# Mean square by a constant weight matrix and row-wide Newton steps in the norms, one batch of indexer scores per query block

## Chip, cores, metric

The kernel runs on one core of one Trainium2 chip. The metric is the device time of a launch in microseconds, as the median over several runs.

## Reference, cut to what matters

Two layers (`DEPTH = 2`) of a hybrid decoder trunk on 256 positions of width 1024, all in float32. Each layer takes a root-mean-square norm, projects, mixes in three branches, adds, takes a second norm and runs a gated feed-forward net:

```python
def rms_norm(x, g):
    r = lax.rsqrt(jnp.mean(xf * xf, axis=-1, keepdims=True) + NORM_EPS)
    return xf * r * g
...
h = rms_norm(x, norm1_g)
proj = h @ w_in                        # q, k, v, iq, ik, iw, a, c, g
y_attn = dsa_attention(q, k, v, iq, ik, iw) @ w_attn_out
y_conf = silu(layer_norm(conv31(a_val * sigmoid(a_gate)), ...)) @ w_conf_out
y_sc = (c_b * conv3(c_c * c_x)) @ w_sc_out
x = x + (sig(g0)*y_conf + sig(g1)*y_attn + sig(g2)*y_sc) @ w_o
u = causal_dwconv(rms_norm(x, norm2_g) @ w_up, ffn_conv_w) + ffn_conv_b
x = x + (silu(u_gate) * u_val) @ w_down
```

The attention picks 64 keys per query by the scores of a small indexer, in query blocks of 128:

```python
rel = relu(einsum('bthd,bsd->bths', iqb, ik))     # 8 indexer heads of width 64
score = einsum('bths,bth->bts', rel, iwb)         # then causal mask and top-k
```

So there are three norms over the 1024 features in a layer: here called a (ahead of `w_in`), c (the LayerNorm of the convolution branch) and b (ahead of `w_up`); the layers are 0 and 1.

## The kernel before, in words

Activations lie feature-major: eight tiles of 128 features by 256 positions (`xres` is the residual). The weights come from memory once, as a stream of 128x2048 chunks (`raw`, 3 buffers), each cut in two halves of 128x1024. Every product is float32 in two parts: ScalarE casts a half to its high part (`wh`, L426), VectorE subtracts that from the whole for the low part (`wl`, L383, both with 6 buffers), and TensorE makes three passes for each 128x128 tile: high times high, low times high, high times the low part of the activations. A matmul is 128x128 weights against 128x256 activations, and 24 of them consume one half. The stages of a layer follow the stream: A (convolution branch, eight pairs of column blocks), IQ, KX, V, Q (indexer and attention projections), C and CB (short convolution), S, then G (gates), T, F (branch outputs), O (`w_o`), U (`w_up`, 22 pairs) and N (`w_down`). The other TensorE work (transposes, indexer scores, attention, norms) is full-precision float32 and is slipped in between these.

The first pairs behind a norm don't wait for it. A pair of stage A or U is multiplied with the un-normalised `xgh`, `xgl` (gain times `xres`) and scaled afterwards (`deferred`, tiles `dA`, `dU`), for the number of pairs that `NDEF` gives: A0 5, A1 3, U0 5, U1 3. From then on the normalised tiles `hh` (high, ScalarE) and `hl` (low, VectorE) are read, which `finish` makes one feature tile at a time from `h = xres * gain * r` on VectorE. At the very start the first two pairs of A are done feature tile by feature tile while the input arrives, and the weights of the first two chunks are split in pieces of 128x512.

`r`, the inverse square root of the mean square plus epsilon, is made by `rsqrt_rows` (L565): TensorE takes the squares `sq` as weights against one column of `avg` (a constant 128x128 matrix of 1/1024), which gives the mean square `ms` with positions on partitions, 128x2. VectorE adds epsilon and takes three Newton steps on 128x2 (`newton_ops`, twelve operations with the shift and the start value, tiles `tv`, `ty`, `tt`, `r2`). TensorE then spreads the result over all partitions, with `r2` broadcast as weights against the identity (`pr`, L572), and ScalarE copies that to `r`. The profile gives a product of 128x128 weights in full precision as four records for two matmuls.

The indexer (loop from L882): for each query block `b` and each half `hq` of the eight heads, four score matmuls go into two banks `is` of two heads each, ScalarE takes the ReLU, and VectorE adds the weighted heads to `sc`. Two such batches per block, four per layer.

What sets the order: nothing is issued in program order. A planner (`Plan`) holds all operations with a cost in ns, the engine and a due time (`G.due`, in most places the running time `clk` of TensorE's stream, shifted by constants), and a list scheduler takes on each engine, when it comes free by these costs, the ready operation with the earliest due time. Operations marked hot (names that begin with a letter of `HOT = "abcqk"`, so all norms) go ahead of others that are ready up to 200 ns sooner. The casts and lows of a weight half are due 9000 ns ahead of their matmuls. Each engine then executes its list in that order; a buffer is handed on when its last reader is planned to be done. So a changed cost moves the order of operations far from the place that was edited.

The lines that matter: L366 issues every matmul, L383 a two-tensor operation of VectorE (`vtt`), L390 one with a scalar and a tensor (`vstt`), L398 and L400 one with a tensor and immediate scalars (`vts`), L421 an activation, L426 a cast.

Of the kernel before, what the change touches and what calls it, by code (L numbers as in the profile page):

```python
# [11 lines left out]
I32 = mybir.dt.int32  # L12
AF = mybir.ActivationFunctionType
ALU = mybir.AluOpType
PSUM = bass.MemoryType.PSUM

P = 128
D = 1024
S = 256
# [6 lines left out]
EPS = 1e-6  # L26
# [110 lines left out]
def ap_of(x):  # L137
    return x.ap() if isinstance(x, View) else x
# [198 lines left out]
def trunk(ctx: ExitStack, tc: tile.TileContext, xt: bass.AP, wst: bass.AP, prm: bass.AP,  # L337
# [7 lines left out]
    G = Plan()  # L345
    clk = {"t": 0.0}

    def width(v):
        if isinstance(v, View) and not v.whole:
            return v.n  # L350
        raise ValueError

    def pe(mms, due=None):
        outs, ins, cost = {}, {}, 0.0
        for o, l, r, st, sp, n, full, kw in mms:
            outs[id(o)] = o
            ins[id(l)] = l
            ins[id(r)] = r
            cost += max(4 * (n / 2.4 + 1.2), 218) if full else max(n, 256) / 2.4 + 2.4

        def fn():
            for o, l, r, st, sp, n, full, kw in mms:
                if kw == "t":
                    nc.tensor.transpose(ap_of(o), ap_of(l), ap_of(r))
                else:
                    nc.tensor.matmul(ap_of(o), ap_of(l), ap_of(r), start=st, stop=sp, skip_group_check=bool(kw))  # L366

        G.add("pe", fn, list(outs.values()), list(ins.values()), cost, due=due)
        return cost

    def mm(o, l, r, st, sp, n, full=False, kw=None):
        return (o, l, r, st, sp, n, full, kw)
# [4 lines left out]
    def psum(v):  # L377
        return isinstance(v, View) and v.buf.tag in BANKS

    def vtt(o, a, b, op, n=None):  # L380
        n = n or width(o)
        c = 62 if psum(a) or psum(b) or psum(o) else 66
        G.add("dve", lambda: nc.vector.tensor_tensor(ap_of(o), ap_of(a), ap_of(b), op=op), [o], [a, b], (c + n) / 0.96)  # L383

    def vstt(o, a, s, b, op0, op1, n=None):
        n = n or width(o)
        c = 62 if psum(a) or psum(b) or psum(o) else 66
        if not isinstance(s, float):
            c += 58
        G.add("dve", lambda: nc.vector.scalar_tensor_tensor(ap_of(o), ap_of(a), ap_of(s), ap_of(b), op0=op0, op1=op1),  # L390
              [o], [a, s, b], (c + n) / 0.96)

    def vts(o, a, s1, s2, op0, op1=None, n=None):
        n = n or width(o)

        def fn():
            if op1 is None:
                nc.vector.tensor_scalar(ap_of(o), ap_of(a), s1, None, op0=op0)  # L398
            else:
                nc.vector.tensor_scalar(ap_of(o), ap_of(a), s1, s2, op0=op0, op1=op1)  # L400

        G.add("dve", fn, [o], [a], (62 + n) / 0.96 if psum(a) else (66 + n / 2) / 0.96)

    def act(o, i, f, scale=None, bias=None, accum=None, n=None):
        n = n or width(o)
        cost = n / 1.2 + (51 if psum(i) else 94)
        kw = {}
        ins = [i]
        outs = [o]
        for k, v in (("scale", scale), ("bias", bias)):  # L410
            if v is not None:
                kw[k] = v
                ins.append(v)
                cost += 93
        if accum is not None:
            kw["accum_out"] = accum
            outs.append(accum)
            cost += 93

        def fn():  # L420
            nc.scalar.activation(ap_of(o), ap_of(i), f, **{k: ap_of(v) for k, v in kw.items()})  # L421

        G.add("act", fn, outs, ins, cost, func=f)
# [16 lines left out]
    def t2(name, dt=F32):  # L440
        return G.buf([P, 2, S], "m2", name, dt)

    def u1(name, dt=F32):
        return G.buf([P, S], "b1", name, dt)

    def t1r(name):
        return G.buf([P, S], "rr", name)
# [68 lines left out]
    avg = G.buf([P, P], "avg", "avg")  # L516

    def const(n):
        o, w = CCOL[n]
        return csb[:, o:o + w]  # L520

    ident = const("ident")
# [15 lines left out]
    for k in range(KD):  # L538
        r, src = (r0, src0) if k < 4 else (r1, src1)
# [8 lines left out]
    def newton_ops(v, y, yi, t, n):  # L548
        vts(yi, v.bitcast(I32), 1, None, ALU.logical_shift_right, n=n)
        vts(yi, yi, -1.0, float(0x5F3759DF), ALU.mult, ALU.add, n=n)  # L550
        cur = yi.bitcast(F32)
        for _ in range(3):
            vtt(t, cur, cur, ALU.mult, n=n)
            vstt(t, t, -0.5, v, ALU.mult, ALU.mult, n=n)
            vstt(y, t, 1.5, cur, ALU.add, ALU.mult, n=n)
            cur = y

    def rsqrt(ss, n, scale, name, keep):
        v = G.buf([P, n], "tv", f"tv{name}")
        yi = G.buf([P, n], "ty", f"ty{name}", I32)  # L560
        t = G.buf([P, n], "tt", f"tt{name}")
        vts(v, ss, scale, EPS, ALU.mult, ALU.add, n=n)
        newton_ops(v, keep, yi, t, n)

    def rsqrt_rows(sq, name):  # L565
        G.hot = name[0] in HOT
        ms = G.buf([P, 2], "pa", f"ms{name}")
        pe([mm(ms[:, b:b + 1], sq[:, b * P:(b + 1) * P], avg[:, 0:1], True, True, 1, True) for b in range(2)])
        r2 = G.buf([P, 2], "r2", f"r2{name}")
        rsqrt(ms, 2, 1.0, name, r2)  # L570
        pr = G.buf([P, S], "pa", f"pr{name}")
        pe([mm(pr[:, b * P:(b + 1) * P], r2[:, b:b + 1].to_broadcast([P, P]), ident, True, True, P, True)  # L572
            for b in range(2)])
        r = t1r(f"r{name}")
        act(r, pr, AF.Copy)
        G.hot = False
        return r

# [176 lines left out]
    for l in range(DEPTH):  # L755
# [38 lines left out]
        ikT = G.buf([P, S], "ikT", f"ikT{l}")  # L794
# [7 lines left out]
        pss = tok(f"IQ{l}", xh, xl, 512, 2)  # L802
        iq = iqb[:, 0:4, :].rearrange("p (b u) d -> p b (u d)", b=2)
        iqT = iqb[:, 4:8, :]
        for b in range(2):
            act(iqb[:, 2 * b:2 * b + 2, :], pss[b].rearrange("p (u d) -> p u d", u=2), AF.Copy)
        pss = tok(f"KX{l}", xh, xl, KX, 2)
# [44 lines left out]
        for g in range(4):  # L852
# [9 lines left out]
            n = g - 1  # L862
# [14 lines left out]
        def spend(ns):  # L877
            paced["t"] += ns * PACE
            G.due = paced["t"]

        for b in range(2):
            nk = (b + 1) * P  # L882
            one = (66 + nk) / 0.96
            sc = G.buf([P, nk], f"sc{b}", f"sc{l}_{b}")
            cur = caus[b]
            for hq in range(2):
                pss = [G.buf([P, 2, nk], "pq", f"is{l}_{b}_{hq}_{i}") for i in range(2)]
                g = []
                for u in range(2):
                    for i in range(2):  # L890
                        q = slice(i * 64, (i + 1) * 64)
                        g.append(mm(pss[i][:, u, :], iqT[q, 2 * hq + u, b * P:(b + 1) * P], ikT[q, :nk],
                                    True, True, nk, True))
                pe(g)
                for i in range(2):
                    rl = G.buf([P, 2, nk], "rel", f"rel{l}_{b}_{hq}_{i}")
                    act(rl, pss[i], AF.Relu)
                    for u in range(2):
                        h = 4 * hq + 2 * u + i
                        vstt(sc, rl[:, u, :], iws[:, b, h:h + 1], cur, ALU.mult, ALU.add)  # L900
                        cur = sc
                        spend(one)
            for r in range(TOPK // 8):
                m8 = G.buf([P, 8], "m8", f"m8{l}_{b}_{r}")
                G.add("dve", lambda m8=m8, sc=sc: nc.vector.max(ap_of(m8), ap_of(sc)), [m8], [sc], one)
                G.add("dve", lambda m8=m8, sc=sc: nc.vector.match_replace(ap_of(sc), ap_of(m8), ap_of(sc), GONE),
                      [sc], [m8, sc], one)
                spend(2 * one)
            vts(bias[b], sc, -2e38, NEG, ALU.is_gt, ALU.mult)
            vtt(bias[b], bias[b], caus[b], ALU.add)  # L910
            spend(2 * one)
# [27 lines left out]
        for b in range(2):  # L939
            nk = (b + 1) * P  # L940
            one = (66 + nk) / 0.96
            bq = slice(b * P, (b + 1) * P)
            for g in range(2):
# [6 lines left out]
                pss = []  # L950
                for hp in range(2):
# [3 lines left out]
                    for i in range(2):  # L955
                        u = 2 * hp + i
# [29 lines left out]
        for n in (1, 2, 0):  # L986
            if n != 2:
                gt[n] = big(f"g{l}_{n}")
            for q in range(4):
# [4 lines left out]
                else:  # L994
                    t = t2(f"g2{l}_{q}")
# [10 lines left out]
        sq = t1r(f"sqc{l}")  # L1006
        for j in range(KD):
            vtt(acc[:, j, :], acc[:, j, :], mu, ALU.subtract)
            t = sq if j == 0 else u1(f"sqc{l}_{j}")
            act(t, acc[:, j, :], AF.Square)  # L1010
            if j:
                vtt(sq, sq, t, ALU.add)
        rc = rsqrt_rows(sq, f"c{l}")
        fh = big(f"cfh{l}", F32R)
        fl = big(f"cfl{l}", F32R)
        for j in range(KD):
            u = u1(f"lu{l}_{j}")
# [187 lines left out]
```

## Time and profile before

| | |
|---|---|
| runs | 1041.38, 1038.53, 1040.28 us |
| median | 1040.28 us |
| the profiled execution: time, span | 1038.84 us, 1037.1 us |
| TensorE, matmul records | 1029.0 us (99%), 8784 |
| VectorE | 911.7 us (88%) |
| ScalarE | 700.7 us (68%) |
| DMA | 191.63 MB, 185 GB/s in the mean |
| granted TensorE clock, mean | 1.0 of full speed |

All views are of one profiled execution, with times from the start of its span. The profile has each engine's busy time, groups of like instructions with the duration of one, and a timeline with the start of each and, in brackets, the idle time ahead of it and what ended it. Matmuls are pipelined: a record of 128x256 lasts 0.28 us and starts 0.11 us behind the one before, so a matmul's cost is the distance between starts. Buffer numbers are left out: `msb` is `ms` of norm b of either layer, and the time tells which.

### The profile page before, as it was taken

The page shows a single profiled execution, that of the slowest core. Times are in us where ns is not written, and L with a number is a line of the kernel's source. Part 1 is how long each engine was busy: PE and PEld are TensorE (multiplying, and loading weights), DVE is VectorE, ACT ScalarE, POOL GpSimd, SP SyncE. Part 2 cuts the span into 40 slices and gives each one's busy share as a digit, 9 for nine tenths or more (in the row PEclk, how much of TensorE's full clock was granted, in tenths as well). Part 3 has the DMA queues.
Part 4 walks back from the last instruction along what each step waited for, and adds up shares of the span by engine and source line. Part 5 has one row for each costly group of instructions (what it writes and reads, how often), then busy time and mean ns, then how long its engine had stood idle before and what let it go on. Part 6 is the DMA issues. An engine that isn't in the chain of part 4 may idle for free.

```text
span 1037.1 us, 21702 instructions
## 1 busy us (share of the span) xinstructions
PE 1029.0 (99%) x8784; PEld 1013.6 (98%) x8784; DVE 911.7 (88%) x1813; ACT 700.7 (68%) x1242; POOL 0.2 (0%) x4
## 2 busy tenths in 40 slices
PE   8999999999999999999999999999999999999998
PEld 7999999999999999999999999999999999999998
DVE  6999999999998899885689999999998889998742
ACT  6868758896665666664466786598958466766531
POOL 0000000000000000000000000000000000000000
PEclk9999999999999999999999999999999999999999
DMA  7664555335665356555545554543464653665560
GB/s 278 241 212 161 175 173 180 127 133 188 218 220 202 135 193 220 202 203 208 172 175 201 203 176 152 203 158 123 162 241 143 228 203 123 221 226 193 182 217 21
DMA packets 29461, 191.63 MB, mean 185 GB/s; under 512 B 3504, under 2 KB 4784, under 8 KB 7088
## 3 DMA queue, kind: packets, MB, share of 16 engines
q1 hardware_dynamic: 29360, 190.23, 52.9%
q8 instruction: 69, 1.13, 0.4%
q14 instruction: 32, 0.26, 0.1%
HBM read 189.17 MB, written 1.05 MB: 183 GB/s over the span
## 4 chain that ended last, share of the span: by engine, by line
PE 96%; DVE 1%; DMA 1%; SPq 0%; issue 0%; ACT 0%; DVEq 0%
PE U L366 23%; PE G L366 13%; PE N L366 12%; PE C L366 9%; PE A L366 6%; PE Q L366 4%; PE T L366 4%; PE S L366 4%; PE CB L366 4%; PE O L366 4%; PE F L366 4%; PE IQ L366 2%; PE KX L366 1%; PE V L366 1%; PE qk L366 1%; PE po L366 1%
## 5 line engine op out<-in xcount | busy, mean ns | idle before, releaser
L383 DVE TENSOR_TENSOR wl<-raw,wh 128x1024 fp32r<-128x1024 f32 (+2 forms) x364 | 432.9, 1199 | 61.9 <-ACT wh L426 60.6
L426 ACT CAST wh<-raw 128x1024 fp32r<-128x1024 f32 (+2 forms) x364 | 368.8, 1029 | 147.5 <-PE N L366 37.2
L366 PE MATMUL U<-hhb,wh 128*128 128x256 f32 x576 | 134.1, 276 | 0.0
L366 PE MATMUL U<-hhb,wl 128*128 128x256 f32 x576 | 134.1, 276 | 0.0
L390 DVE SCALAR_TENSOR_TENSOR acc<-a,psb,acc 128x245 f32<-128x245 f32 (+18 forms) x320 | 132.3, 463 | 0.1
L366 PEld LDWEIGHTS U<-hhb,wl 128*128 128x128 f32 x576 | 108.1, 188 | 0.0
L366 PEld LDWEIGHTS U<-hhb,wh 128*128 128x128 f32 x576 | 108.1, 188 | 0.0
L366 PE MATMUL G<-hha,wh 128*128 128x256 f32 x384 | 91.0, 279 | 0.0
L366 PE MATMUL G<-hha,wl 128*128 128x256 f32 x384 | 89.7, 276 | 0.0
L366 PE MATMUL N<-uh,wh 128*128 128x256 f32 x352 | 80.7, 276 | 0.0
L366 PE MATMUL N<-uh,wl 128*128 128x256 f32 x352 | 80.7, 276 | 0.0
L366 PE MATMUL U<-hlb,wh 128*128 128x256 f32 x576 | 77.0, 276 | 0.0
L366 PEld LDWEIGHTS G<-hha,wl 128*128 128x128 f32 x384 | 72.1, 188 | 0.3 <-issue 0.2
L366 PEld LDWEIGHTS G<-hha,wh 128*128 128x128 f32 x384 | 72.1, 188 | 0.3 <-issue 0.2
L390 DVE SCALAR_TENSOR_TENSOR u<-U,psb,u 128x255 f32<-128x255 f32 (+1 forms) x144 | 59.7, 475 | 14.5 <-ACT u L421 14.4
L366 PEld LDWEIGHTS U<-hlb,wh 128*128 128x128 f32 x576 | 70.6, 188 | 0.0
L421 ACT ACTIVATE ct<-a,psb 128x253 f32<-128x253 f32 (+9 forms) x160 | 70.1, 490 | 0.0
L366 PEld LDWEIGHTS N<-uh,wh 128*128 128x128 f32 x352 | 66.1, 188 | 0.0
L366 PEld LDWEIGHTS N<-uh,wl 128*128 128x128 f32 x352 | 66.1, 188 | 0.0
L366 PE MATMUL C<-hha,wh 128*128 128x256 f32 x256 | 61.0, 280 | 0.0
L366 PE MATMUL C<-hha,wl 128*128 128x256 f32 x256 | 59.9, 276 | 0.0
L421 ACT ACTIVATE u<-U,psb 128x256 f32<-128x256 f32 x72 | 37.2, 560 | 27.5 <-PE U L366 27.4
(259 smaller groups left out, 2563.1 us busy)
## 6 DMA issues: line engine op xcount, KB each, us to landing
raw<-in_w SPq DMA_DIRECT2D x174, 1024.0 KB, 4.8
raw<-in_w SPq DMA_DIRECT2D x4, 656.0 KB, 3.9
raw<-in_w SPq DMA_DIRECT2D x8, 256.0 KB, 6.0
out<-xres SPq DMA_DIRECT2D x8, 128.0 KB, 2.2
xres<-in_xt SPq DMA_DIRECT2D x3, 256.0 KB, 6.8
psb<-in_p SPq DMA_DIRECT2D x2, 277.0 KB, 6.8
csb<-in_c SPq DMA_DIRECT2D x1, 304.0 KB, 7.6
xres<-in_xt SPq DMA_DIRECT2D x2, 128.0 KB, 3.6
```

What stands on the lines that cost most here:

```text
L366: nc.tensor.matmul(ap_of(o), ap_of(l), ap_of(r), start=st, stop=sp, skip_group_check=bool(kw))
L383: G.add("dve", lambda: nc.vector.tensor_tensor(ap_of(o), ap_of(a), ap_of(b), op=op), [o], [a, b], (c + n) / 0.96)
L390: G.add("dve", lambda: nc.vector.scalar_tensor_tensor(ap_of(o), ap_of(a), ap_of(s), ap_of(b), op0=op0, op1=op1), [o], [a, s, b], (c + n) / ...
L421: nc.scalar.activation(ap_of(o), ap_of(i), f, **{k: ap_of(v) for k, v in kw.items()})
L426: G.add("act", lambda: nc.scalar.copy(ap_of(o), ap_of(i)), [o], [i], width(o) / 1.2 + 94)
```

## The change

The mean square is now one matmul with `avg` as the weights and `sq` as the moving operand, so that every partition of a bank 128x256 gets the mean square of every position. VectorE's Newton steps run on 128x256 and write `r` directly; the spreading product and ScalarE's copy are gone. In the indexer, a block's eight score matmuls are one batch: for block 0 in two banks of four heads, for block 1 in four banks of two heads, two of them from the banks `pa`; ReLU takes a whole bank each.

```diff
--- before.py
+++ after.py
@@ -564,15 +564,14 @@
 
     def rsqrt_rows(sq, name):
         G.hot = name[0] in HOT
-        ms = G.buf([P, 2], "pa", f"ms{name}")
-        pe([mm(ms[:, b:b + 1], sq[:, b * P:(b + 1) * P], avg[:, 0:1], True, True, 1, True) for b in range(2)])
-        r2 = G.buf([P, 2], "r2", f"r2{name}")
-        rsqrt(ms, 2, 1.0, name, r2)
-        pr = G.buf([P, S], "pa", f"pr{name}")
-        pe([mm(pr[:, b * P:(b + 1) * P], r2[:, b:b + 1].to_broadcast([P, P]), ident, True, True, P, True)
-            for b in range(2)])
+        ms = G.buf([P, S], "pa", f"ms{name}")
+        pe([mm(ms, avg, sq, True, True, S, True)])
         r = t1r(f"r{name}")
-        act(r, pr, AF.Copy)
+        v = G.buf([P, S], "nv", f"nv{name}")
+        yi = G.buf([P, S], "ny", f"ny{name}", I32)
+        t = G.buf([P, S], "nt", f"nt{name}")
+        vts(v, ms, 1.0, EPS, ALU.mult, ALU.add)
+        newton_ops(v, r, yi, t, S)
         G.hot = False
         return r
 
@@ -883,20 +882,24 @@
             one = (66 + nk) / 0.96
             sc = G.buf([P, nk], f"sc{b}", f"sc{l}_{b}")
             cur = caus[b]
+            per = 4 if b == 0 else 2
+            pss = [[G.buf([P, per, nk], "pa" if c else "pq", f"is{l}_{b}_{c}_{i}") for i in range(2)]
+                   for c in range(4 // per)]
+            g = []
             for hq in range(2):
-                pss = [G.buf([P, 2, nk], "pq", f"is{l}_{b}_{hq}_{i}") for i in range(2)]
-                g = []
                 for u in range(2):
                     for i in range(2):
                         q = slice(i * 64, (i + 1) * 64)
-                        g.append(mm(pss[i][:, u, :], iqT[q, 2 * hq + u, b * P:(b + 1) * P], ikT[q, :nk],
+                        n = 2 * hq + u
+                        g.append(mm(pss[n // per][i][:, n % per, :], iqT[q, n, b * P:(b + 1) * P], ikT[q, :nk],
                                     True, True, nk, True))
-                pe(g)
+            pe(g)
+            for c in range(4 // per):
                 for i in range(2):
-                    rl = G.buf([P, 2, nk], "rel", f"rel{l}_{b}_{hq}_{i}")
-                    act(rl, pss[i], AF.Relu)
-                    for u in range(2):
-                        h = 4 * hq + 2 * u + i
+                    rl = G.buf([P, per, nk], "rel", f"rel{l}_{b}_{c}_{i}")
+                    act(rl, pss[c][i], AF.Relu)
+                    for u in range(per):
+                        h = 2 * (per * c + u) + i
                         vstt(sc, rl[:, u, :], iws[:, b, h:h + 1], cur, ALU.mult, ALU.add)
                         cur = sc
                         spend(one)
```

The planner counts the Newton steps with their larger costs and so orders other work anew. Three places, row by row in the order of issue (a name is the tile with its planner number; `ha0_3` is the feature tile 3 of the normalised `h` of norm a, layer 0):

VectorE at the start, behind the last Newton step of norm a of layer 0, in the kernel before:

```order
L390 SCALAR_TENSOR_TENSOR r2a0_350<-tta0_343,r2a0_350 128x2
L383 TENSOR_TENSOR wl3_322<-raw1_189,wh3_309 128x512
L383 TENSOR_TENSOR wl4_371<-raw2_267,wh4_338 128x1024
L383 TENSOR_TENSOR wl5_383<-raw2_267,wh5_357 128x1024
L383 TENSOR_TENSOR wl6_403<-raw3_311,wh6_375 128x1024
L390 SCALAR_TENSOR_TENSOR ha0_0_413<-xres_171,n1g_154,ra0_401 128x256
L390 SCALAR_TENSOR_TENSOR ha0_1_423<-xres_171,n1g_154,ra0_401 128x256
L390 SCALAR_TENSOR_TENSOR ha0_2_427<-xres_171,n1g_154,ra0_401 128x256
L383 TENSOR_TENSOR hla0_440<-ha0_0_413,hha0_425 128x256
L383 TENSOR_TENSOR hla0_440<-ha0_1_423,hha0_425 128x256
```

and in the changed one:

```order
L390 SCALAR_TENSOR_TENSOR ra0_362<-nta0_347,ra0_362 128x256
L383 TENSOR_TENSOR wl3_322<-raw1_190,wh3_310 128x512
L383 TENSOR_TENSOR wl4_375<-raw2_268,wh4_336 128x1024
L383 TENSOR_TENSOR wl5_385<-raw2_268,wh5_353 128x1024
L390 SCALAR_TENSOR_TENSOR ha0_0_398<-xres_172,n1g_155,ra0_362 128x256
...
L383 TENSOR_TENSOR hla0_423<-ha0_4_440,hha0_410 128x256
L383 TENSOR_TENSOR hla0_423<-ha0_5_451,hha0_410 128x256
L390 SCALAR_TENSOR_TENSOR ha0_6_468<-xres_172,n1g_155,ra0_362 128x256
L383 TENSOR_TENSOR wl6_470<-raw3_312,wh6_366 128x1024
L383 TENSOR_TENSOR hla0_423<-ha0_6_468,hha0_410 128x256
L383 TENSOR_TENSOR wl7_476<-raw3_312,wh7_370 128x1024
```

The low of the half `wl6` stood ahead of all `ha0` and now stands behind seven of them and six `hla0`, next to `wl7`.

ScalarE behind norm b of layer 1 (`hhb1` are the normalised high parts, `u1_0` the first pair of U; `wh303` to `wh305` are halves of `w_up`), before:

```order
L421 ACTIVATE hhb1_11627<-hb1_0_11613 128x256
L421 ACTIVATE hhb1_11627<-hb1_1_11615 128x256
L421 ACTIVATE hhb1_11627<-hb1_2_11625 128x256
L421 ACTIVATE hhb1_11627<-hb1_3_11629 128x256
L426 CAST wh303_11657<-raw151_11469 128x1024
L421 ACTIVATE hhb1_11627<-hb1_4_11660 128x256
L421 ACTIVATE hhb1_11627<-hb1_5_11673 128x256
L421 ACTIVATE hhb1_11627<-hb1_6_11685 128x256
L421 ACTIVATE u1_0_0_11699<-dU1_0_11670,psb1_6426 128x256
L421 ACTIVATE u1_0_1_11710<-dU1_0_11670,psb1_6426 128x256
L421 ACTIVATE hhb1_11627<-hb1_7_11697 128x256
L426 CAST wh304_11724<-raw152_11534 128x1024
```

and in the changed kernel:

```order
L426 CAST wh303_11591<-raw151_11428 128x1024
L421 ACTIVATE hhb1_11607<-hb1_0_11580 128x256
...
L421 ACTIVATE hhb1_11607<-hb1_4_11609 128x256
L426 CAST wh304_11635<-raw152_11492 128x1024
L421 ACTIVATE hhb1_11607<-hb1_5_11649 128x256
L421 ACTIVATE hhb1_11607<-hb1_6_11659 128x256
L426 CAST wh305_11674<-raw152_11492 128x1024
L421 ACTIVATE u1_0_0_11680<-dU1_0_11639,psb1_6403 128x256
L421 ACTIVATE u1_0_1_11682<-dU1_0_11639,psb1_6403 128x256
L421 ACTIVATE hhb1_11607<-hb1_7_11678 128x256
```

The cast of `wh303` stood behind four `hhb1` and now stands ahead of all; those of `wh304` and `wh305` stood behind the last `hhb1` and now stand ahead of the activations of `u1_0` and of that last one.

ScalarE behind norm a of layer 1, at the end of its `hha1`, before:

```order
L426 CAST wh189_7218<-raw94_7080 128x1024
L421 ACTIVATE hha1_7188<-ha1_4_7221 128x256
L421 ACTIVATE hha1_7188<-ha1_5_7234 128x256
L421 ACTIVATE hha1_7188<-ha1_6_7246 128x256
L421 ACT_TABLE_LOAD
L421 ACTIVATE sg1_0_7260<-dA1_0_7231 128x256
L421 ACTIVATE hha1_7188<-ha1_7_7258 128x256
L421 ACTIVATE sg1_1_7284<-dA1_1_7271 128x256
```

and in the changed kernel:

```order
L421 ACTIVATE hha1_7186<-ha1_4_7188 128x256
L426 CAST wh190_7214<-raw95_7102 128x1024
L421 ACTIVATE hha1_7186<-ha1_5_7228 128x256
L421 ACTIVATE hha1_7186<-ha1_6_7238 128x256
L426 CAST wh191_7253<-raw95_7102 128x1024
L421 ACT_TABLE_LOAD
L421 ACTIVATE sg1_0_7259<-dA1_0_7218 128x256
L421 ACTIVATE hha1_7186<-ha1_7_7257 128x256
```

The cast of `wh191` now stands ahead of the table load, the first sigmoid `sg1_0` and the last `hha1`.

## Rows read from the trace of the kernel before

**Rows 1.** Page: busy time by engine, TensorE's granted clock in 40 slices

```profile
PE 1029.0 (99%) x8784; PEld 1013.6 (98%) x8784; DVE 911.7 (88%) x1813; ACT 700.7 (68%) x1242; POOL 0.2 (0%) x4
...
PEclk9999999999999999999999999999999999999999
```

**Rows 2.** Timeline, TensorE, layer 0's FFN norm: start, us, engine, line, operation, out<-in

```profile
345.97 0.50 PE L366 MATMUL msb<-avg,sqb 128*128 128x1 f32 x4
346.33 1.07 PE L366 MATMUL U<-xglb,wh 128*128 128x256 f32 x7
...
349.62 0.28 PE L366 MATMUL U<-xghb,wl 128*128 128x256 f32 x1
349.73 0.60 PE L366 MATMUL prb<-csb,r2b 128*128 128x128 f32 x4
...
351.10 0.28 PE L366 MATMUL U<-xghb,wh 128*128 128x256 f32 x1
```

**Rows 3.** Timeline, VectorE, start of the kernel, first mixer norm

```profile
18.21 0.15 DVE L400 TENSOR_SCALAR tva<-msa 128x2 f32<-128x2 f32 x1
...
20.45 4.10 DVE L383 TENSOR_TENSOR wl<-raw,wh 128x512 fp32r<-128x512 f32 x4
```

**Rows 4.** Timeline, TensorE, start of the kernel

```profile
1.04 4.64 PE L366 MATMUL pw<-avg 128*128 128x128 f32 x20 [1.04 <-DVE avg L526]
...
21.20 0.73 PE L366 MATMUL A<-xgha,wl 128*128 128x256 f32 x4 [1.03 <-DVE wl L383]
...
22.22 0.60 PE L366 MATMUL pra<-csb,r2a 128*128 128x128 f32 x4
...
36.64 0.28 PE L366 MATMUL A<-xgha,wh 128*128 128x256 f32 x1
```

**Rows 5.** Timeline, VectorE, layer 1's FFN norm

```profile
857.75 0.16 DVE L400 TENSOR_SCALAR tvb<-msb 128x2 f32<-128x2 f32 x1 [1.22 <-PE msb L366]
...
873.64 1.22 DVE L383 TENSOR_TENSOR wl<-raw,wh 128x1024 fp32r<-128x1024 f32 x1
```

**Rows 6.** Timeline, TensorE, layer 1, behind its mixer norm and its FFN norm

```profile
541.31 0.28 PE L366 MATMUL A<-hha,wh 128*128 128x256 f32 x1
...
872.09 0.28 PE L366 MATMUL U<-hhb,wh 128*128 128x256 f32 x1
...
876.06 0.28 PE L366 MATMUL U<-hhb,wl 128*128 128x256 f32 x1
```

**Rows 7.** Timeline, TensorE, mean product of layer 0's LayerNorm

```profile
266.71 1.02 PE L366 MATMUL mu<-am,avg 128*128 128x256 f32 x4
...
267.69 0.28 PE L366 MATMUL G<-hha,wl 128*128 128x256 f32 x1
```

**Rows 8.** Timeline, TensorE, a score batch of layer 0's indexer

```profile
113.17 1.07 PE L366 MATMUL C<-hla,wh 128*128 128x256 f32 x8
114.17 0.72 PE L366 MATMUL is<-ikT,iq 64*128 64x128 f32 x8
```

**Rows 9.** Groups by line and form, VectorE: busy us, mean ns, idle before

```profile
L390 DVE SCALAR_TENSOR_TENSOR hb<-xres,psb,rb 128x256 f32<-128x256 f32 x16 | 7.1, 477 | 0.0
...
L383 DVE TENSOR_TENSOR sqb<-sqb,sqb 128x256 f32<-128x256 f32 x14 | 5.9, 418 | 0.0
...
L400 DVE TENSOR_SCALAR bias<-sc 128x256 f32<-128x256 f32 x2 | 0.6, 284 | 0.0
```

**Rows 10.** Timeline, ScalarE, layer 1, behind its mixer norm and its FFN norm

```profile
534.54 1.05 ACT L426 CAST wh<-raw 128x1024 fp32r<-128x1024 f32 x1 [0.44 <-PE A L366]
...
537.25 1.28 ACT L421 ACT_TABLE_LOAD   x1
538.54 0.42 ACT L421 ACTIVATE sg<-dA 128x256 f32<-128x256 f32 x1
...
865.32 1.05 ACT L426 CAST wh<-raw 128x1024 fp32r<-128x1024 f32 x1 [0.44 <-PE U L366]
...
867.92 1.08 ACT L421 ACTIVATE u<-dU,psb 128x256 f32<-128x256 f32 x2
```

## Prediction

> **What bounds the kernel now.** I read the page first, then TensorE's waits, then the timelines around the six norms and the indexer. TensorE is busy 99% of the span [rows 1]: the steady step is 0.113 us per matmul (349.62 to 349.73 [rows 2]), eight in 0.91, and after the first 35 us it waits nowhere. So a change has two ways to the time: what it takes from or adds to TensorE's own work, and whether it makes a weight half or a normalised tile arrive later than TensorE wants it. VectorE has 88%, so its work counts only where its lead is short. A lead is the end of an operand's writer against the start of the first matmul that reads it. At the start there is none: TensorE stands 1.03 us at 21.20 for the low half written at 20.45 [rows 3, 4]. Behind the FFN norms it is 1.2 us: a low half of layer 1 runs from 873.64 to 874.86 [rows 5], its matmul starts at 876.06 [rows 6]; layer 0 has the same pattern. The other operands behind a norm's product lead by 2.0 us or more.
>
> **TensorE's own work.** A norm's old products: from the spreading product to the end of the eight matmuls behind it pass 1.37 us (349.73 to 351.10 [rows 2]), less their own 0.91 is 0.46. The mean square takes 0.36 to the next matmul [rows 2] and, as behind the other, 0.09 in what follows. Together 0.91. The new product is one 128x256 full-precision matmul with avg as weights. The mean product of the LayerNorm has that form: two of them and one matmul take 0.98 (266.71 to 267.69 [rows 7]), less 0.11 is 0.87, so 0.44 for one. Saved, to a hundredth: 0.46 per norm, on the path in five norms: **-2.3** (the sixth is inside the start, below).
>
> The indexer: a batch makes the matmuls ahead of it 0.09 longer (the eight from 113.17 take 1.00 until 114.17 [rows 8]), and I take as much behind it as behind the spreading product. Its products stay; four batches fewer, 0.18 each: **-0.7**. The banks that the merged batch needs were read long before, so I take no wait. Its activations, fewer and longer, and the six copies of the spread row that go are on ScalarE (68% busy) and cost or give nothing.
>
> **VectorE's new chain.** The old one is twelve dependent operations on 128x2, one per 0.2 us: 18.21 to 20.45 until the next low half can start, 2.24 [rows 3]. None on 128x256 with immediate scalars is in the trace. Nearest rows: a two-tensor operation of that size takes 0.418, one with a scalar column 0.477, a one-source operation from SBUF 0.284 [rows 9]. Between dependent ones the old chain leaves 0.035 (2.24 / 12, less 0.15). I take 0.415 for the first (it reads PSUM) and the nine two-tensor ones, 0.284 for the shift and the multiply-add: 10 x 0.45 + 2 x 0.32, less 0.1 for the overlap of the last with an independent one: **5.0 us, 2.8 more**. Ends: 3.9 if all run at 0.284, 5.7 at 0.477 with integers at 0.415. For the integer steps the trace has only narrow tiles.
>
> The Trainium skill (VectorE: DVE Perf Modes, "Mode 2×_2P — use both read ports for one tensor") says that a one-source operation within SBUF makes two results a cycle, and two-tensor operations never do. Rows 9 agree on fp32 (0.284 against 0.418), no run here shows it on integers; by the rule the sum is the one below, without it for integers each chain is 0.26 longer and the sum 1.0 higher.
>
> What the chain gives back: pr's wait and the copy go, but ha starts no earlier, since the chain itself ends where the copy did.
>
> **Start (layer 0, mixer norm).** The chain stands ahead of the second low piece of the half that TensorE waits for. Now that piece starts at 18.21 + 5.0 = 23.2 and TensorE goes on at 23.97 instead of 21.20 (0.75 behind its start, as before). It finishes A_0 and A_1 after 1.02 (21.20 to 22.22 [rows 4]) at 25.0, and two halves of A_2, 24 matmuls or 2.72 us each, at 30.4. The third half's low moved: it is now behind seven ha (0.40 each) and six hla (0.33; both are rows 9 less the 0.08 by which independent neighbours overlap). VectorE: four lows in 4.10 were [rows 3], now three, until 26.15; plus 4.8 is 30.95, plus 1.22 is 32.2. TensorE wanted it at 30.5: 1.7 more. Two halves on, A_4's second half starts at 40.3; it was 36.64 [rows 4]. **+3.6**, the saved spreading product included.
>
> **FFN norms (b0, b1).** In layer 1, Newton starts at 857.75 and the critical low half at 873.64 [rows 5]: 15.9 us, of which 2.24 chain, 0.16 a wait, 13.5 other work in one unbroken row. Now: 857.84 (the product's last pass ends 0.09 later by rows 7) + 5.0 + 13.5 - 0.34 (one product moved behind) = 876.0. To this come waits for ScalarE. All four casts now stand ahead of the first hhb, and the last of them waits for a weight buffer that TensorE frees (865.32, now 0.46 earlier [rows 10]): hhb comes 0.25 late. The cast of wh305 waits two halves, 5.44, longer (870.3) and stands ahead of the two activations of U_0 (1.0 together [rows 10]), for which VectorE waits another 0.4; hhb_7 follows at 872.7, where TensorE wants it at 872.09 - 0.46 [rows 6]. That wait (1.1) lies inside the next: the low ends at 877.9 and is wanted at 876.06 - 0.46 = 875.6. Stall 2.3 in each layer: **+4.6**.
>
> **Mixer norm of layer 1 (a1).** Here hha is needed from A_3 on. Now the cast of wh191 stands ahead of the table load, sg_0 and hha_7. Its buffer comes free two halves after that of wh189 (534.54 - 0.46), at 539.5; cast 1.05, table load 1.28, sg_0 0.4, hha_7 0.4 [rows 10]: 542.6. TensorE wants it at 541.31 - 0.46 [rows 6]. **+1.8**.
>
> **LayerNorms (c0, c1).** Leads of the halves and of cfl behind them are over 4 us, VectorE has holes a few us later: nothing but the 0.46. Transposes and products of the attention change place by up to 16 matmuls (1.8 us); ScalarE's steps move with them, so zero, at most +1 in all. SyncE's loads follow the lows; the load of the fifth chunk is issued 2.8 later, and its cast, behind six hha, later too.
>
> **Sum.** -2.3 - 0.7 + 3.6 + 4.6 + 1.8 = **+7.0** on the profiled execution, 1038.84 (its span 1037.1, and 1.7 around it): 1045.8. The median of the three runs is 1.4 higher; between both bases I put 1046.5. Ends: with the chain at 3.9 each of the four stalls loses 1.1, +2.5 in all; at 5.7 they gain 0.7 each, and the attention's 1.0: +10.7.
>
> **Rivals.** (1) *All the longer chains hide*: the time is then TensorE's saving alone, six norms at 0.46 and 0.7: 1038.84 - 3.5 = **1035.3**. It decides if VectorE's debt stays below the leads, 1.2 us, that is if a 128x256 step costs under 0.3. For it: most halves lead by over 3 us; against: no lead at the start, and 0.418 in rows 9. Chance 0.05. (2) *Only the start pays*: behind b0, b1 and a1 the debt is taken up because the casts now run earlier and VectorE finds holes: +3.6 - 2.3 - 0.7, **1039.4**. Against: the 13.5 us without a hole, and hhb behind casts that wait for TensorE. Chance 0.14. (3) *The clock falls at the start.* TensorE would stand from 20.17 to 23.97, 3.8 us where it was 1.03. The granted clock shows the full level, 2.4 GHz, throughout [rows 1], but the warm-up products at the very start take 0.21 us per 128 columns and more (20 in 4.64 us [rows 4]), the 1.2 GHz level, twice what the spreading product's four add later (0.46 [rows 2]). A stretch at the slow level as long as that first row and the 0.7 behind it, 5.3 us, would cost half of itself, 2.6, of which the 1.7 at the third half hide most: +1.0 on my forecast, **1047.5**. The Trainium skill (TensorE: Matmul & The Clock Gate, "What's actually happening") says that the slow level is the default and that idleness brings it back; by that rule this rival is the case, and the row of warm-up products agrees only for the start. Chance 0.15.
>
> **Numbers.** My forecast has 0.66. A measurement of this kernel tells 0.3%, 3.1 us, from no change. Rivals 1 and 2 lie below that, and of the forecast's own spread a little: faster 0.05, same 0.18, slower 0.77. The range goes from just under rival 2 to the upper end of the costs (1038.84 + 10.7, and half of the 1.4 between the bases), 1039 to 1050.
>
> **What would show it.** Newton's lines at 128x256 near 0.45 us per step; TensorE waiting for wl near 24 and 32 us, for hha near 541 and for wl 18 us behind each FFN norm's product, with 2 us each; no wait behind the LayerNorms; clock full throughout. Wrong if TensorE shows no wait behind the FFN norms, if steps take 0.3, or if new waits stand in the attention.

## Result and the profile after

| | before | changed |
|---|---|---|
| median | 1039.96 us (4 runs, 1038.53 to 1041.38) | 1048.22 us (4 runs: 1047.65, 1047.98, 1048.45, 1057.54) |
| median, repeated beside the last experiments | 1039.52 us (15 runs) | 1047.36 us (5 runs, 1047.02 to 1048.10) |
| ratio, 95% interval | | 1.0102 [1.0079, 1.0126]; repeated 1.0077 [1.0064, 1.0089] |
| profiled execution: time, span | 1038.84, 1037.1 | 1057.54, 1055.8; repeated 1047.74, 1045.9 |

The change makes the kernel slower, by 8.3 us in the medians and 7.8 in the repetition (some 0.8%; both intervals lie above 1). The profiled execution of the first measurement is one of its own, 9 us above all the others; what it has in addition is shown below. The waits of TensorE in it:

```profile
PE A L366 <- ACT xgha L421: 3.5, 2, 2.9
PE A L366 <- DVE wl L383: 3.4, 1, 3.4
PE U L366 <- DVE wl L383: 2.3, 2, 2.2
PE A L366 <- ACT hha L421: 1.6, 1, 1.6
...
PE U L366 <- ACT hhb L421: 0.9, 1, 0.9
PE U L366 <- DVE hlb L383: 0.5, 1, 0.5
```

(Columns: us in total, times, longest.) Before, TensorE stood 1.0 for a low half [rows 4] and 2.5 for the input at the start, and not behind any later norm. Now it stands for a low half at the start (3.4), for a low half behind the first FFN norm (2.2), for the last `hha` of layer 1 (1.6) and for `hhb`, `hlb` and a low behind the second FFN norm (1.6 together). The wait for `xgha` is one for input that lands at different times in every execution; it is also there in experiments that leave the first norm old (2.7 with the indexer's part alone). In both profiles of the changed kernel the granted clock is 0.50 for some 3 us behind it (13 to 16 us in this one); so it is in five of the twelve others.

VectorE's chain, timeline of the first norm in the changed kernel, answers to [rows 3]:

```profile
19.30 0.42 DVE L400 TENSOR_SCALAR nva<-msa 128x256 f32<-128x256 f32 x1 [0.57 <-PE msa L366]
19.76 0.29 DVE L398 TENSOR_SCALAR nya<-nva 128x256 int32<-128x256 int32 x1
...
20.42 0.43 DVE L383 TENSOR_TENSOR nta<-nya 128x256 f32<-128x256 f32 x1
...
24.44 2.96 DVE L383 TENSOR_TENSOR wl<-raw,wh 128x512 fp32r<-128x512 f32 x3
```

and TensorE there, which answers to [rows 4]:

```profile
18.68 0.59 PE L366 MATMUL msa<-sqa,avg 128*128 128x256 f32 x2
...
25.18 0.75 PE L366 MATMUL A<-xgha,wl 128*128 128x256 f32 x4 [3.39 <-DVE wl L383]
```

The chain lasts 5.14 us (19.30 to 24.44) where it lasted 2.24: steps of 0.46, and 0.33 for the two integer ones. In this execution VectorE also waits 0.57 for the product ahead of it, which TensorE reached late at the lower clock; in the repeated one it does not wait there.

Where the time went is read best from matched matmuls, the first of a stage, in the repeated profile (span 1045.9, which agrees with the medians). TensorE's timeline of the changed kernel, repeated:

```profile
60.16 0.39 PE L366 MATMUL IQ<-wh,hha 128*128 128x512 f32 x1
...
345.19 0.28 PE L366 MATMUL U<-xghb,wh 128*128 128x256 f32 x1
...
469.40 0.28 PE L366 MATMUL N<-uh,wh 128*128 128x256 f32 x1
...
529.24 0.28 PE L366 MATMUL A<-xgha,wh 128*128 128x256 f32 x1
...
575.14 0.39 PE L366 MATMUL IQ<-wh,hha 128*128 128x512 f32 x1
...
860.17 0.28 PE L366 MATMUL U<-xghb,wh 128*128 128x256 f32 x1
...
982.74 0.28 PE L366 MATMUL N<-uh,wh 128*128 128x256 f32 x1
```

Before, the same matmuls start at 55.68, 341.99, 462.62, 522.46, 566.93, 853.24 and 973.87, and the difference runs +4.48, +3.20, +6.78, +6.78, +8.21, +6.93, +8.87. So, by place: start +4.5; indexer and LayerNorm -1.3 in each layer; first FFN norm +3.6; mixer norm of layer 1 +1.4; second FFN norm +1.9. Stages without a norm or the indexer differ by nothing.

Not all of the 4.5 at the start is the change's. VectorE's last square of the input and, for the kernel before, the first matmul of stage IQ:

```profile
16.48 0.41 DVE L383 TENSOR_TENSOR sqa<-sqa,sqa 128x256 f32<-128x256 f32 x1
...
55.68 0.39 PE L366 MATMUL IQ<-wh,hha 128*128 128x512 f32 x1
```

and the same square and the first Newton operation in the repeated profile:

```profile
17.16 0.42 DVE L383 TENSOR_TENSOR sqa<-sqa,sqa 128x256 f32<-128x256 f32 x1
...
18.89 0.42 DVE L400 TENSOR_SCALAR nva<-msa 128x256 f32<-128x256 f32 x1
```

The square comes 0.68 later, ahead of anything that was changed, and so does Newton's first operation (18.89, before 18.21 [rows 3]). From that operation to stage IQ pass 41.27 us, before 37.47: 3.8 is the change's own loss. The profiles of the first measurement and of the norms alone give the same, 41.29 and 41.31.

### The profile page after: what moved, and what is told of

Read it like the earlier page. It is cut to its first block, busy times and chain, and to the rows that moved or that the text cites. A ratio compares the mean times of both kernels' runs of the same rounds, so it can differ in the third digit from the quotient of the medians.

```text
span 1055.8 us, 21602 instructions
## 1 busy us (share of the span) xinstructions
PE 1039.2 (98%) x8748; PEld 1024.6 (97%) x8748; DVE 928.0 (88%) x1813; ACT 696.7 (66%) x1230; POOL 0.2 (0%) x4
## 4 chain that ended last, share of the span: by engine, by line
PE 96%; DVE 2%; DMA 1%; ACT 1%; SPq 0%; issue 0%; ACTq 0%; DVEq 0%
PE U L366 22%; PE G L366 12%; PE N L366 12%; PE C L366 8%; PE A L366 8%; PE Q L366 4%; PE S L366 4%; PE CB L366 4%; PE T L366 4%; PE O L366 4%; PE F L366 4%; PE IQ L366 2%; PE KX L366 1%; PE V L366 1%; PE qk L366 1%; PE po L366 1%
## 5 line engine op out<-in xcount | busy, mean ns | idle before, releaser
L366 PE MATMUL U<-hhb,wh 128*128 128x256 f32 x576 | 137.7, 279 | 0.9 <-ACT hhb L421 0.9
L366 PE MATMUL U<-hhb,wl 128*128 128x256 f32 x576 | 137.7, 279 | 0.2 <-DVE wl L383 0.2
L390 DVE SCALAR_TENSOR_TENSOR acc<-a,psb,acc 128x251 f32<-128x251 f32 (+16 forms) x320 | 132.7, 462 | 0.1
L366 PEld LDWEIGHTS U<-hhb,wh 128*128 128x128 f32 x576 | 108.2, 188 | 1.1 <-ACT hhb L421 1.1
L366 PEld LDWEIGHTS U<-hhb,wl 128*128 128x128 f32 x576 | 108.2, 188 | 0.4 <-DVE wl L383 0.4
L366 PE MATMUL G<-hha,wh 128*128 128x256 f32 x384 | 92.1, 282 | 0.0
L366 PE MATMUL G<-hha,wl 128*128 128x256 f32 x384 | 89.7, 276 | 0.0
L366 PE MATMUL N<-uh,wh 128*128 128x256 f32 x352 | 83.0, 279 | 0.0
L366 PE MATMUL N<-uh,wl 128*128 128x256 f32 x352 | 83.0, 279 | 0.0
L366 PE MATMUL U<-hlb,wh 128*128 128x256 f32 x576 | 79.1, 279 | 0.5 <-DVE hlb L383 0.5
L366 PEld LDWEIGHTS G<-hha,wl 128*128 128x128 f32 x384 | 72.1, 188 | 1.0 <-issue 0.7
L366 PEld LDWEIGHTS G<-hha,wh 128*128 128x128 f32 x384 | 72.1, 188 | 1.0 <-issue 1.0
L366 PEld LDWEIGHTS U<-hlb,wh 128*128 128x128 f32 x576 | 72.3, 188 | 0.7 <-DVE hlb L383 0.7
L366 PEld LDWEIGHTS N<-uh,wl 128*128 128x128 f32 x352 | 66.1, 188 | 0.0
L366 PEld LDWEIGHTS N<-uh,wh 128*128 128x128 f32 x352 | 66.1, 188 | 0.0
L366 PE MATMUL C<-hha,wh 128*128 128x256 f32 x256 | 60.5, 279 | 0.0
L366 PE MATMUL C<-hha,wl 128*128 128x256 f32 x256 | 59.9, 276 | 0.0
```

## Experiments

### The parts alone

The indexer's loop alone (the second half of the diff):

> Only the indexer's part of the change; norms as before. In the changed kernel's profile the stage with the score products gains 0.8 us in each layer. Theory (the norms' longer VectorE chain is the whole loss): 1.6 us less than before, about 1038.3, no new wait on TensorE. Rival by the forecast's smaller term: 0.7 less, 1039.3. Rival that the merged batch waits for its banks: above 1040 with a wait of TensorE at the score products.

Measured: 1037.95 us against 1039.48 (ratio 0.9986 [0.9977, 0.9995]), 1.5 less. The merged batch, TensorE's timeline:

```profile
126.37 0.28 PE L366 MATMUL C<-hha,wl 128*128 128x256 f32 x1
126.58 2.00 PE L366 MATMUL is<-ikT,iq 64*128 64x256 f32 x16
128.51 0.38 PE L366 MATMUL C<-hha,wh 128*128 128x256 f32 x1
128.73 0.28 PE L366 MATMUL C<-hha,wl 128*128 128x256 f32 x1
```

From 126.37 to 128.73 pass 2.36, less two ordinary steps 2.13. Before, a batch of half the size in the same block took 126.61 to 128.11 by the same pairs, 1.50, less two steps 1.27. Two of those are 2.54: a batch less is worth 0.41, and no wait came. The smaller term falls.

The norms alone (the first half of the diff):

> Only the norms' part; indexer as before. Theory: the change's loss plus what the indexer gave back, 1048.2 + 1.6 = 1049.8, with waits of TensorE at the start (over 3 us) and behind both FFN norms and the second mixer norm (near 2 us each). Rival (the indexer's part carries a share of the loss): under 1047.

Measured: 1047.65 us (1.0076 [1.0063, 1.0090]), with the waits of the change, 3.9 at the start among them. It is some 2 less than the sum wanted, 1049.8. In its profile the granted clock stayed full behind the first FFN norm (the difference to before grows there by 2.0, not 3.6), and the input came earlier (stage IQ +4.1, not +4.5).

### The order told with the old costs

```diff
-        vts(v, ms, 1.0, EPS, ALU.mult, ALU.add)
-        newton_ops(v, r, yi, t, S)
+        vts(v, ms, 1.0, EPS, ALU.mult, ALU.add, n=2)
+        newton_ops(v, r, yi, t, 2)
```

The last argument is only the size from which the planner's cost is made; the work is the same.

> The whole change, but the planner is told the Newton steps' old costs (two columns), so casts and lows keep nearly the old order and only the chain is longer. Theory (the length of the chain, 5.1 instead of 2.2 us, is what TensorE waits for): the start's and the FFN norms' waits stay, 1046 to 1049. Rival (the moved order, casts ahead of the normalised tiles, is the cause): those waits go, 1036 to 1040. At the second mixer norm, where the moved cast was named as the cause, the wait of 1.8 falls to 1.3 or less.

Measured: 1047.05 us (1.0070 [1.0054, 1.0085]), 0.3 to 1.2 less than the change. The waits at the start (3.4) and behind the FFN norms stay. The one for `hha` falls from 1.6 to 1.0, as the moved cast of `wh191` wanted. So far this spoke, at the start and the FFN norms, for the chain's length and against the order.

### The LayerNorms alone

```diff
+    def rsqrt_rows(sq, name):
+        return (rsqrt_new if name[0] == "c" else rsqrt_old)(sq, name)
```

(`rsqrt_old` and `rsqrt_new` are the two forms of `rsqrt_rows`; the indexer is merged.)

> The indexer's part, and the new norm for the two LayerNorms alone; mixer and FFN norms as before. Theory: both give TensorE time and no wait, 2 x 0.8 + 2 x 0.48 = 2.6 less than before, 1037.4. Rival (any 2.9 us more on VectorE makes some half late): a wait of TensorE behind the LayerNorms, 1039 or more.

Measured: 1036.91 us (0.9974 [0.9964, 0.9984]), 2.6 less than before and faster than both kernels. No wait behind a LayerNorm: their leads cover the chain.

### A shorter and a longer chain

`newton_ops` with two steps, or four, instead of three (with two, r is a little less exact):

> The whole change with two Newton steps instead of three, so r is a little less exact and the chain three operations of 0.46, 1.4 us, shorter. Theory (each of the four waits is the chain less a fixed lead): the waits at the start, behind both FFN norms and behind the second mixer norm fall by 1.4 each, from 3.4, 2.2, 2.4 and 1.6, and no slow clock behind the first FFN norm: 1041 to 1043. Rival (a chain on 128x256 costs its waits through the moved casts, whatever its length): above 1046.

> The whole change with a fourth Newton step, 1.4 us more chain. Theory: 1.4 more at each of the same four places and nothing behind the LayerNorms, whose leads are over 4 us: 1048.2 + 5.5 = 1053.7, up to 3 more if the slow clock comes behind more of the waits. Rival (the waits are set by something else, casts or loads): within 2 of the change, 1046 to 1050.

Measured: 1038.28 us with two steps (0.9988 [0.9978, 0.9997]) and 1049.60 with four (1.0095 [1.0080, 1.0110]). Both theories miss (the run with four steps lies in its rival's range), and in a way that the chain's length alone cannot give: 1.4 us less of it per norm took 9 to 10 us, 1.4 more added 1.4 to 2.2. With two steps TensorE waits behind no norm but the first; the whole answer of the waits' view:

```profile
PE A L366 <- ACT xgha L421: 3.6, 2, 2.6
PE A L366 <- DVE wl L383: 3.3, 2, 2.0
PE pw L366 <- DVE avg L526: 1.0, 1, 1.0
```

The orders of the two runs explain it. Behind an FFN norm the low half that TensorE waits for (`wl122` in layer 0, `wl302` in layer 1) is the 31st operation of VectorE behind the chain in the change, the 32nd before and with the old costs, but the 27th with two and with four steps: the planner, with other costs, puts it ahead of operations of the second U pair, not behind them. In layer 1 the start of that low comes 13.5 us after the chain's end in the kernel before and with the old costs, 13.65 in the change, but 11.6 with two and four steps. So when the low comes, behind an FFN norm, is set by the chain's length and by the work that stands between the two. With four steps the two nearly cancel there: matched matmuls lose 1.3 and 1.8 at the FFN norms (3.6 and 1.9 in the change), while the mixer norm of layer 1 loses 3.7 (1.4) and the start, counted from Newton's first operation, 2.0 more.

### The good order with three steps

```diff
-        newton_ops(v, r, yi, t, S)
+        newton_ops(v, r, yi, t, 120)
```

> The whole change with its three Newton steps, but the planner is given smaller costs for them (as for 120 columns), which gives the order of the run with two steps: behind the FFN norms the critical low of a weight half stands ahead of five operations of the second U pair instead of behind them, and the casts of wh125, wh191 and wh305 stand later. Theory now (the waits behind the FFN norms are the chain plus the place that the planner gave the low): with the leads of the run with two steps (low of layer 0's half 1.1 us, last hhb of layer 1 0.05, last hha of layer 1 0.35) and 1.4 more chain, waits of 0.3 behind norm b0, 1.0 behind a1 and 1.3 behind b1, the start as in the change: 1042 to 1043.5. Rival (only the chain's length counts, as forecast): waits as in the change, 1046 to 1048.

Measured: 1040.64 us (1.0016 [1.0007, 1.0025]), below both theories and 6.7 less than the repeated change, by a number that no instruction sees. VectorE behind the second FFN norm, the change:

```profile
874.58 0.42 DVE L400 TENSOR_SCALAR nvb<-msb 128x256 f32<-128x256 f32 x1 [1.30 <-PE msb L366]
...
888.60 0.48 DVE L390 SCALAR_TENSOR_TENSOR u<-dU,psb,u 128x255 f32<-128x255 f32 x1 [0.27 <-ACT u L421]
...
889.61 1.26 DVE L390 SCALAR_TENSOR_TENSOR u<-dU,psb,u 128x255 f32<-128x255 f32 x3
...
893.37 1.21 DVE L383 TENSOR_TENSOR wl<-raw,wh 128x1024 fp32r<-128x1024 f32 x1
```

and with the steered order:

```profile
858.73 0.42 DVE L400 TENSOR_SCALAR nvb<-msb 128x256 f32<-128x256 f32 x1 [1.30 <-PE msb L366]
...
875.43 1.22 DVE L383 TENSOR_TENSOR wl<-raw,wh 128x1024 fp32r<-128x1024 f32 x1
876.57 1.66 DVE L390 SCALAR_TENSOR_TENSOR u<-dU,psb,u 128x255 f32<-128x255 f32 x4
```

From Newton's first operation to the critical low pass 18.8 us in the change and 16.7 here: the low stands four operations earlier, which is worth about the 1.66 that four operations of the second pair take, and VectorE no longer waits 0.27 for ScalarE ahead of it. TensorE's waits in this run:

```profile
PE A L366 <- DVE wl L383: 3.9, 1, 3.9
PE A L366 <- ACT xgha L421: 2.6, 2, 2.1
PE pw L366 <- DVE avg L526: 1.0, 1, 1.0
PE U L366 <- ACT hhb L421: 0.2, 1, 0.2
PE A L366 <- ACT hha L421: 0.2, 1, 0.2
```

The start is as bad as in the change, and the three later norms have 0.2 or less each. In this order the casts of `wh191` and of the `w_up` halves also stand later, and how much that is worth, at the mixer norm above all, was not taken apart. In matched matmuls the steered order gives back 3.7 at the first FFN norm (the granted clock stays full there), 1.4 at the mixer norm of layer 1 and 1.5 at the second FFN norm.

### The first norm, and the clock behind its wait

The change with the first norm in the old form:

> The whole change, but the first norm (layer 0, mixer) computed the old way. Theory: the start's loss of 4.1 goes and the waits behind the FFN norms and the second mixer norm stay: 1044.1, the wait at the start back at 1.0 or less. Rival (the later waits are a late effect of the start): under 1041.

Measured: 1043.14 us (1.0032 [1.0019, 1.0045]); the low half's wait at the start is back at 1.0, the later ones are those of the change. So the start's loss is its own, 4.2 by the medians against the repeated change and 4.0 by the two spans (1045.9 - 1041.9).

The change with unused products of `avg` behind the last matmuls ahead of the wait, seven and then eleven of them:

```diff
+                    free = 7 if k == KD - 1 and part == 0 and j == 1 else 0
+                    if free:
+                        pd = G.buf([P, P], "pa", "pd")
+                        g += [mm(pd, avg, avg, True, True, P, True) for i in range(free)]
-                    clk["t"] += pe(g, due=clk["t"])
+                    clk["t"] += pe(g, due=clk["t"], free=free)
```

(`pe` leaves the last `free` products out of the planner's cost.)

> The whole change, with seven products of the constant matrix (3.2 us, their result unused) put on TensorE ahead of the low half that it waits for at the start, so that it works where it would stand idle. Forecast's reading (the slow clock after that wait hides a wait at the third half that would come anyway): clock full behind the wait, a new wait of 1.3 to 1.7 at the third half, total 1047.5 to 1048.5. Rival (the slow clock is paid in full): no new wait, 1.6 less, 1046.5.

> As the run with seven unused products at the start, but with eleven (5 us), so that TensorE works until the low half is there. Forecast's reading (the slow clock hides a wait that comes anyway): clock full behind it, a wait of 1 to 1.7 at the third half, the same time as the change, 1047.5 to 1048.5. Rival (the slow clock costs its 1.6 in full): no wait at the third half, 1046.5.

With seven, 1047.80 us (1.0078 [1.0063, 1.0093]): a wait of 1.8 was left and the clock fell all the same, so this run told nothing on the question. With eleven, 1046.98 (1.0070 [1.0054, 1.0085], four runs from 1045.8 to 1048.4, too wide apart to decide by their median). TensorE's timeline of that run (its lines are one higher, L367 for L366):

```profile
25.02 0.74 PE L367 MATMUL A<-xgha,wl 128*128 128x256 f32 x4 [0.94 <-DVE wl L384]
...
33.22 0.39 PE L367 MATMUL A<-xgha,wl 128*128 128x256 f32 x1 [1.32 <-DVE wl L384]
```

and two windows of it, then the same two of the repeated change (us, then busy time and count of PE, PEld, DVE, ACT, POOL, then the granted clock, DMA share, GB/s):

```profile
25.00:30.00 5.00, 4.98 (x42) 4.97 (x43) 5.00 (x10) 1.35 (x4) 0.00 (x0) 1.00 0.77 269
30.00:36.00 6.00, 4.68 (x41) 4.49 (x40) 6.00 (x12) 5.26 (x9) 0.00 (x0) 1.00 0.41 139
```

```profile
25.00:30.00 5.00, 5.00 (x30) 4.99 (x30) 5.00 (x11) 1.61 (x5) 0.00 (x0) 0.66 0.83 316
30.00:36.00 6.00, 6.00 (x55) 6.00 (x54) 6.00 (x12) 5.26 (x9) 0.00 (x0) 1.00 0.30 104
```

The clock stays full behind the first wait, 42 matmuls instead of 30 pass in 25 to 30, and 41 instead of 55 in 30 to 36: a wait of 1.3 stands at the third half. From Newton's first operation to stage IQ pass 41.31 us, against 41.27 in the repeated change: the slow clock there was free, since the third half's low, behind the `ha` and `hla`, sets the end.

### A version from what was found

The indexer in one batch; the new norm with the steered costs everywhere but in the first norm, which stays old; one more pair deferred in layer 1:

```diff
-NDEF = {"A0": 5, "A1": 3, "U0": 5, "U1": 3}
+NDEF = {"A0": 5, "A1": 4, "U0": 5, "U1": 4}
...
-        newton_ops(v, r, yi, t, S)
+        newton_ops(v, r, yi, t, 120)
...
+    def rsqrt_rows(sq, name):
+        return (rsqrt_new if name != "a0" else rsqrt_old)(sq, name)
```

> A version put together from these runs: indexer in one batch; the new norm everywhere but in the first norm, which stays old; the planner given the smaller costs; in layer 1 one more pair deferred behind each norm (four instead of three). Theory: no wait over 0.5 behind any norm; TensorE's savings of 1.6 (indexer) and five norms at 0.48, less up to 0.8 of small waits: 1036 to 1037, under 1036.9 if no new wait comes. Rival (the extra deferred pairs' work on VectorE, 0.7 each, turns into waits of low halves): 1038 or more.

Measured: 1035.71 us (1035.14 to 1036.40, five runs; ratio 0.9965 [0.9952, 0.9977]), the fastest of all. TensorE's waits, all that the view lists:

```profile
PE A L366 <- ACT xgha L421: 1.2, 2, 0.6
PE pw L366 <- DVE avg L526: 1.0, 1, 1.0
PE A L366 <- DVE wl L383: 1.0, 1, 1.0
```

Its lead over the version with the LayerNorms alone, 1.2 us in the medians, is inside what the two intervals leave open.

### The change once more

> The change itself once more, to see whether its profiled time of 1057.5 returns. Theory (that execution had matmul steps of 0.120 instead of 0.113 us for 170 us, which is nothing that the change does): all runs at 1047.5 to 1049. Rival (the change brings that step about in a fixed share of its runs): one run in four near 1057.

Measured: 1047.02 to 1048.10, median 1047.36 us (1.0077 [1.0064, 1.0089]). The 1057.5 did not return, so it was one run in nine. What that execution had more is seen in two windows (columns as above), from behind the wait at the first FFN norm to the next norm. The first profile:

```profile
370.00:375.00 5.00, 4.72 (x27) 4.72 (x28) 5.00 (x10) 2.16 (x4) 0.00 (x0) 0.66 0.48 151
375.00:543.00 168.00, 168.00 (x1403) 168.00 (x1402) 125.81 (x207) 97.80 (x152) 0.00 (x0) 1.00 0.55 191
```

The repeated one:

```profile
370.00:375.00 5.00, 5.00 (x31) 5.00 (x32) 5.00 (x10) 2.13 (x5) 0.00 (x0) 0.66 0.55 187
375.00:543.00 168.00, 168.00 (x1483) 167.95 (x1482) 133.79 (x227) 101.54 (x160) 0.00 (x0) 1.00 0.56 197
```

In both the granted clock falls behind the wait. Then it is full again in both, but the first makes 80 matmuls fewer in 168 us: a step of 0.120 us instead of 0.113, worth 80 x 0.113 = 9.1 us. It lasts until the next norm's full-precision product, at 543.0.

## Why the prediction was right or wrong

The sign and the medians were right: 1046.5 forecast, 1048.2 and 1047.4 measured, inside 1039 to 1050. The ratio of all runs, 1.0102, is 1050.6 on its before and lies above the range, by the one execution with the long steps.

- **The step that failed** is "clock full throughout". The sum took TensorE's pace, 0.113 us per matmul, as given, and put what the clock does behind a wait at nothing, apart from a rival at the start. The runs showed two things in its place. Behind the first FFN norm the granted clock fell (windows 0.66, 3.4 us at twice the step, 1.7 us lost), in six of the seven profiles that have that wait of 2.0 to 2.2, and there nothing hides it. And the execution that lies above the range made 1403 matmuls at 0.120 us from the moment that the clock was back behind that wait, some 9 us more, for which no term of the sum and no end of the range had room. What brings the long step is open. The Trainium skill (TensorE: Matmul & The Clock Gate, "What's actually happening") speaks of idleness bringing the slow level back, and these rows agree in so far as each fall follows a wait of TensorE.
- **The clock rival** had the place and the price off. At the start the clock fell in all six profiles with a wait of 3.4 to 5.3 for the low half. With three Newton steps that cost nothing, as the fill showed (41.31 against 41.27). With four steps the slow level lasted 6.8 us, and the start lost 2.0 more than in the change for 1.4 more chain.
- **TensorE's own work** was right for the norms: 0.46 a norm forecast, 0.46 and 0.49 measured by matched matmuls at the two LayerNorms. The indexer was mis-sized: 0.18 a batch was taken from the spreading product, it is 0.41, so -1.6 instead of -0.7.
- **VectorE's chain**: 5.0 forecast, 5.14 measured. The integer steps on 128x256 take 0.29, as the Trainium skill has it for one source within SBUF (VectorE: DVE Perf Modes, "Mode 2×_2P — use both read ports for one tensor"); the trace now shows it on integers too.
- **Start**: +3.6 forecast, 3.8 measured from Newton's first operation (0.14 of the rest is the chain's length). The wait at the third half was there as forecast, once the clock did not hide it.
- **FFN norms**: a wait of 2.3 less the product's 0.46, 1.8 each, was forecast. The second loses 1.9; the first loses 2.0 in the profile of the norms alone, where the clock stayed full, and 3.6 in the change.
- **Mixer norm of layer 1**: 1.8 less 0.46, 1.3, forecast, 1.4 measured; with the old costs, and the cast in another place, 0.9.
- **What the forecast had right for this order alone**: it read the order of the changed kernel and priced the chain in it. By its sum the critical low behind the second FFN norm starts 18.8 us after Newton's first operation, and it does. But the work between chain and low, 13.65 us here, is the planner's choice: with 11.6 of it the same chain costs 6.7 us less in the whole kernel. Rival 2, only the start pays, is what the steered order comes to, and its time, 1039.4, is near the 1040.6 measured.

The terms as measured in the repeated profile: 3.8 + 3.6 + 1.4 + 1.9 - 1.6 - 0.95 = 8.2, where the forecast had 7.0. With 0.7 for the later input that is the 8.9 by which the span ends later. That the sum came so near is in part luck: the clock's 1.7 behind the first FFN norm, put at nothing, and the 0.9 that the indexer gave back beyond its term go against each other.

## What to carry to other kernels

A longer chain on an engine with 88% load is priced by its length together with the work that stands between it and the next critical operation: list that work, and see whether the order can be changed before the chain is. Behind a planner that works on costs, a few runs with those costs varied, work unchanged, tell how much of a result is its order. A change that works at several places of different lead should be tried place by place: here it gains at two norms and loses at four. And before a loss at the start is put down to a change, see when the input came in both executions.

## What the runs showed of the hardware that was not expected

- After the clock came back behind a wait, TensorE ran 1403 matmuls at 0.120 us each instead of 0.113, at a granted clock of 1.00, until the next full-precision product. The same step shows for short stretches at the start of other profiles, where the granted clock is 1.00 as well: in the kernel before from 6.6 to 7.8 us, with the indexer's part alone from 14.0 to 16.6. What sets it is open.
- The clock does not follow the length of one wait alone: it stayed full behind the 2.2 at the first FFN norm in the run with the norms alone, and behind the 1.6 at layer 1's mixer norm in all six profiles that have it, but fell behind the 1.8 that seven unused products had left, and behind the two waits of layer 1's mixer norm, 1.9 together, in the run with four steps.
- A two-tensor operation on 128x256 with an immediate scalar takes 0.425, as the plain one (0.418 [rows 9]); with a scalar column it was 0.477.
